# Contractions over 64 sample tokens widened to 128 rows in a hybrid encoder layer

## The chip, the core and the metric

The kernel runs on one core of a Trainium2 chip. The engines that matter here are TensorE (PE; PEld is the loading of its stationary operand, which is a separate instruction), VectorE (DVE), ScalarE (ACT), GpSimd (POOL) and SyncE (SP), which issues most of the DMAs. The metric is the device time of one execution in microseconds (us), as the median over several runs. "Rows" of a matmul are the partitions over which it contracts, "columns" the width of its stationary operand: a form such as `64*128 64x258` means 64 rows, 128 stationary columns and 258 streamed columns.

## What is computed

One layer over 256 prompt tokens and 64 sample tokens, in float32. Only the parts with a contraction over tokens matter here:

```python
def step(carry, xs):                      # mLSTM, block by block, 4 heads
    ...
    s = jnp.einsum('bhtd,bhsd->bhts', qb, kb) * jnp.exp(d - m_t[..., None])
    num = (w_inter[..., None] * jnp.einsum('bhtd,bhde->bhte', qb, C)
           + jnp.einsum('bhts,bhse->bhte', s, vb))
    ...
    C_new = decay[..., None, None] * C + jnp.einsum('bhs,bhsd,bhse->bhde', ws, kb, vb)
    n_new = decay[..., None] * n + jnp.einsum('bhs,bhsd->bhd', ws, kb)

def token_mix(...):
    ...
    zr = zs.reshape(B, nch, lc, N_GROUPS_S, GS_W)          # lc = 128 prompt, 64 sample
    mix = (jnp.einsum('gts,bnsge->bntge', w_s, zr) + ...)
    y_s = (u * mix.reshape(B, S, D_S)).astype(h.dtype)
    out = jnp.concatenate([y_m, y_s], axis=-1) @ w_out

def layer(...):
    x = x + mix
    hid = jnp.square(jax.nn.relu(rmsnorm(x, g_norm2) @ w_ff1))
    x = x + hid @ w_ff2
```

## The kernel before

Activations lie feature-major, 128 features on the partitions and 320 tokens along them (256 prompt tokens, then 64 sample tokens). Weights are the stationary operand. Each float32 operand of a projection is split into a high and a low part and a product is carried by three passes, so one output tile of 128 features takes 48 matmuls of 320 columns (`Job.matmuls`, L86 to L97): two halves of 16 (L93, L94) and 8 (L97).

The program is one list of jobs, one per output tile: 8 of z, 4 of q, 8 of v, 8 of o, 8 of u, 16 of the output projection (`out`), then four times 16 of the first and 16 of the second feed-forward matrix. All engines run what was recorded for them in the order of the code; nothing reorders it. Ahead of a job's matmuls `run_side` advances what was put off with `later`: the side work of earlier jobs, which is where all small matmuls stand. So PE's stream is: a few small matmuls, 48 projection matmuls, a few small ones, and so on. Weight halves are loaded four ahead (SP) and split two jobs ahead (ACT writes the high part, DVE the low part).

The small matmuls take the tokens in three groups, `TOK = ((0, 128), (128, 128), (256, 64))`. The third group is the sample, 64 tokens. They are:

- `z_side` (L382): transposes gz to token-major (`zt`, L391), normalises, and keeps the result in zs; zs[2] is the sample's, 64 rows of one half of the tile z2g. The other half of z2g, zs[3], takes a gain vector by DMA. z2g has a slot that held input tiles (xraw) before.
- `mix` (L413, called ahead of each u job): for each of 8 channel tiles three matmuls into one PSUM tile (L417), the third over the sample's 64 rows. They are float32, so each is two passes on PE.
- `v_side` (L448): transposes v (`vt`, L452) and splits it into vau_h and vau_l, 128 x 3 x 258, two buffers each; the third slice is the sample's, 64 rows.
- `head` (L464), one per head, in three steps with jobs between them. Step one makes the scores S (L467 to L469) and transposes k (`kt`, L472), and ACT and DVE make from them the operands Ph, Pl (448 columns, the last 64 the sample's) and kh, kl (three slices). Step two multiplies them with v (`mv`, three passes by L496 to L498): into T[0] and T[1] for the prompt; into T[2] for the sample, after a matmul of qi with the old state C0 (L507); into cs for the prompt's new state, and cs2 for the sample's. Then DVE and ACT make a normalised output hmt (L532). Step three transposes hmt back to feature-major (`hT`, L543), two halves of three transposes, the third of each over the sample's 64 rows.

Ph, Pl, kh, kl and hmt are taken from a pool with one buffer in each head. POOL sums the squares of the input early (until 42.3 us), then fills some constants (L238 to L242), sums the squares of z (L375, L378, one per z job), and makes qi.

Of the kernel before, what the change touches and what calls it, by code (L numbers as in the profile page):

```python
"""mLSTM / spatial-gating hybrid encoder layer on one core.

Activations stay feature-major ([128 features, k tile, 320 tokens]); weights are the
stationary operand. Every float32 operand of a projection is split exactly into two
float32r parts (12 significant bits each) and a product is carried by three passes
(hi*hi + hi*lo + lo*hi), accumulated in float32 in PSUM.
"""
# [10 lines left out]
F32 = mybir.dt.float32  # L18
F32R = mybir.dt.float32r
AF = mybir.ActivationFunctionType  # L20
ALU = mybir.AluOpType
PSUM = bass.MemoryType.PSUM
DRAM = bass.MemoryType.DRAM

P = 128
# [3 lines left out]
NS = 64  # L29
NT = NP + NS  # L30
H = 4
DV = 256
VA = DV + 1
VP = DV + 2
# [12 lines left out]
def emit(tc, A):  # L47
    nc = tc.nc
    act, dve, pe, pool, sp = nc.scalar, nc.vector, nc.tensor, nc.gpsimd, nc.sync
# [17 lines left out]

# [1 line left out]
    class Job:  # L69
# [28 lines left out]

# [1 line left out]
    cst = cp.tile([P, 64], F32, name="cst")  # L100
# [16 lines left out]
    def rsqrt_to(out, ss, n, tmp, tag):  # L117
        """out = (ss / n) ** -0.5, one Newton step after the table."""
        r0, t = tmp(tag + "r"), tmp(tag + "t")
        act.activation(r0, ss, AF.Abs_reciprocal_sqrt, scale=1.0 / n)  # L120
        dve.tensor_tensor(t, r0, r0, ALU.mult)
        dve.scalar_tensor_tensor(t, ss, -0.5 / n, t, ALU.mult, ALU.mult)
        dve.scalar_tensor_tensor(out, t, 1.5, r0, ALU.add, ALU.mult)

    ap_ctx = ExitStack()
    ap = ap_ctx.enter_context(tc.tile_pool(name="phase_a", bufs=1))
# [4 lines left out]

    # slots of the later Y operands that hold early intermediates
    def yslot(part, k, name, dt=F32):
# [5 lines left out]

# [1 line left out]
    nchunk = (KT + XC - 1) // XC  # L141
# [24 lines left out]
    ident = cp.tile([P, P], F32, name="ident")  # L166
# [9 lines left out]
    for k in range(KT):  # L176
# [10 lines left out]
        hi = wp.tile([P, W0], F32R, tag="hi", name=f"w0hi{k}")  # L187
        lo = wp.tile([P, 4 * P], F32R, tag="lo", name=f"w0lo{k}")
# [17 lines left out]
        first, last = k == 0, k == KT - 1  # L206
# [8 lines left out]

    # remaining constants of the first part
    C0 = ap.tile([P, H, VP], F32, name="C0")
# [8 lines left out]

# [1 line left out]
    qT = [yslot("h", 8 + h, f"qT{h}") for h in range(H)]  # L228
# [8 lines left out]
    for i in range(2):  # L237
        pool.memset(vau_h[i].bitcast(F32)[:, :, DV:VA], 1.0)  # L238
        pool.memset(vau_h[i].bitcast(F32)[:, :, VA:], 0.0)
        pool.memset(vau_l[i].bitcast(F32)[:, :, DV:], 0.0)  # L240
    gmT = ap.tile([P, 3, 36], F32, name="gmT")
    pool.memset(gmT[:], 0.0)  # L242
# [19 lines left out]
    def split_to(dst, k, src):  # L262
        """dst[k] = (hi, lo) of the float32 tile src, in the Y slots."""
        h_ = yslot("h", k, f"Yh{k}", F32R)
        l_ = yslot("l", k, f"Yl{k}", F32R)
        act.copy(h_[:], src)  # L266
        dve.tensor_tensor(l_[:], src, h_.bitcast(F32)[:], ALU.subtract)  # L267
        dst[k] = (h_, l_)

# [1 line left out]
    def row(i, name, n=4):  # L271
# [93 lines left out]

# [1 line left out]
    def z_evac(c):  # L367
# [14 lines left out]
    def z_side(c, gz):  # L382
        if c == 0:
            z01 = ap.tile([P, 2, 8, P], F32, tag="big", name="z01", bufs=2)
            z2g = ap.tile([P, 2, 8, P], F32, tag="big", name="z2g", bufs=2)
            zs[:] = [z01[:, 0], z01[:, 1], z2g[:, 0], z2g[:, 1]]
            zs.append(z01)
            sp.dma_start(zs[3], A["gsgu"].partition_broadcast(P))
        pt = sdt(f"zt{c}")
        for j, (t0, n) in enumerate(TOK):  # L390
            pe.transpose(pt[:n, P * j:P * j + P], gz[:, t0:t0 + n], ident[:])  # L391
        dve.tensor_copy(zs[4][:, :, c, :], pt[:, 0:256].rearrange("p (j c) -> p j c", c=P))
        dve.tensor_copy(zs[2][:NS, c, :], pt[:NS, 256:384])
        if c < 7:
            return
        yield
        st = sdt("ssz")
        for j, (t0, n) in enumerate(TOK):
            pe.matmul(st[:n, 2 * j:2 * j + 2], sacc[:, t0:t0 + n], ones[:, 0:2], start=True, stop=True)
        s3 = small(P, 3)("z3s")  # L400
        pool.memset(s3, 1.0)
        for j, (t0, n) in enumerate(TOK):
            dve.tensor_copy(s3[:n, j:j + 1], st[:n, 2 * j:2 * j + 1])
        rsqrt_to(rz[:], s3, D // 2, small(P, 3), "rz")
        for j, (t0, n) in enumerate(TOK):
            yield
            dve.scalar_tensor_tensor(zs[j][:n], zs[j][:n], rz[:n, j:j + 1], zs[3][:n],
                                     ALU.mult, ALU.mult)
        sp.dma_start(A["zs_out"], zs[2][:NS])
# [3 lines left out]
    def mix(c):  # L413
        g = c // 2
        pt = sdt(f"mix{c}")
        for j, (t0, n) in enumerate(TOK):
            pe.matmul(pt[:, t0:t0 + n], zs[j][:n, c, :], wsp[:n, g, :n], start=True, stop=True)  # L417
        m = tmp320(f"mixb{c}")
        dve.tensor_tensor(m[:, 0:128], pt[:, 0:128], bsp[:, g, :], ALU.add)
        dve.tensor_tensor(m[:, 128:256], pt[:, 128:256], bsp[:, g, :], ALU.add)  # L420
        dve.tensor_tensor(m[:, 256:NT], pt[:, 256:NT], bsp[:, g, :NS], ALU.add)
        mixb[c] = m
# [9 lines left out]

# [1 line left out]
    def q_evac(h):  # L434
# [29 lines left out]
    def head(h):  # L464
# [14 lines left out]
        pool.tensor_tensor(qi[:], q[:, NP:], eb[:, 192:256], ALU.mult)  # L479
        Ph = ap.tile([P, 448], F32R, tag="Ph", name=f"Ph{h}", bufs=1)  # L480
        Pl = ap.tile([P, 448], F32R, tag="Pl", name=f"Pl{h}", bufs=1)
        for n, c in ((P, slice(0, 384)), (NS, slice(384, 448))):
            act.copy(Ph[:n, c], Pm[:n, c])
            dve.tensor_tensor(Pl[:n, c], Pm[:n, c], Ph.bitcast(F32)[:n, c], ALU.subtract)
        kh = ap.tile([P, 3, P], F32R, tag="kh", name=f"kh{h}", bufs=1)
        kl = ap.tile([P, 3, P], F32R, tag="kl", name=f"kl{h}", bufs=1)
        for j, (n, e, c) in enumerate(((128, ea, 255), (128, eb, 127), (64, eb, 191))):
# [7 lines left out]
        def mm3(out, wh, wl, xh, xl, start, stop):  # L495
            pe.matmul(out, wh, xh, start=start, stop=False)  # L496
            pe.matmul(out, wh, xl, start=False, stop=False)
            pe.matmul(out, wl, xh, start=False, stop=stop)  # L498

        def mv(out, wh, wl, sl, n, j, start, stop):  # L500
            mm3(out, wh[(slice(0, n),) + sl], wl[(slice(0, n),) + sl], vh[:n, j, :], vl[:n, j, :],
                start, stop)

        mv(T[0][:, :VP], Ph, Pl, (slice(0, 128),), P, 0, True, True)
        mv(T[1][:, :VP], Ph, Pl, (slice(128, 256),), P, 0, True, False)
        mv(T[1][:, :VP], Ph, Pl, (slice(256, 384),), P, 1, False, True)
        pe.matmul(T[2][:NS, :VP], qi[:], C0[:, h, :], start=True, stop=False)  # L507
        mv(T[2][:NS, :VP], Ph, Pl, (slice(384, 448),), NS, 2, False, True)
        cs = sdt(f"cs{h}")
        mv(cs[:, :VP], kh, kl, (0,), P, 0, True, False)  # L510
        mv(cs[:, :VP], kh, kl, (1,), P, 1, False, True)
        cs2 = sdt(f"cs2{h}")
        mv(cs2[:, :VP], kh, kl, (2,), NS, 2, True, True)
        sm = small(P, 3)
# [14 lines left out]
        dve.tensor_tensor(rs, rs, den, ALU.mult)  # L529
        hmt = ap.tile([P, 3, DV], F32, tag="hm", name=f"hm{h}", bufs=1)  # L530
        for j, (t0, n) in enumerate(TOK):
# [8 lines left out]
        for e in range(2):  # L540
            pt = sdt(f"hT{h}_{e}")
            for j, (t0, n) in enumerate(TOK):
                pe.transpose(pt[:, t0:t0 + n], hmt[:n, j, e * P:e * P + P], ident[:n, :n])  # L543
            t = yslot("h", 2 * h + e, f"hmT{h}_{e}")
            act.activation(t[:], pt[:, :NT], AF.Copy, scale=gmh(2 * h + e))
            hm[h] = hm[h] or [None, None]
            hm[h][e] = t
# [18 lines left out]

# [1 line left out]
    jobs = []  # L568
# [17 lines left out]

# [1 line left out]
    xres = [None] * KT  # L588
# [111 lines left out]

# [1 line left out]
    job, xl = jobs[-1], xres[KT - 1]  # L702
# [59 lines left out]
    k = 0  # L762
# [95 lines left out]
```

## Time and profile before

| | |
|---|---|
| time, median of three runs | 1371.12 us (1370.93 to 1371.53) |
| profiled execution: span from first to last instruction | 1368.3 us |
| outside the span, against the median | 2.8 us |
| PE busy | 99% of the span, 9197 matmul passes |
| DVE, ACT, POOL busy | 50%, 39%, 4% |
| DMA | 207 MB, 151 GB/s over the span |

Of the profiled execution the profile gives the span alone; its own full time is not known, so the span is compared with the median of the runs. In the timelines a row has a start, a length (from the first start to the last end of what is merged in it), the engine, the line, the operation and the form. Consecutive matmuls overlap in the pipeline: a pass has a duration of about 0.27 to 0.31 us, and the next starts 0.11 to 0.15 us after it. So the pace of PE is read from start to start.

### The profile page before, as it was taken

Reading aid. Unit: us, or ns where it says so; the run is one execution under the profiler, and the core shown is the slowest. Engines: PE = TensorE matmul, PEld = TensorE weight load, DVE = VectorE, ACT = ScalarE, POOL = GpSimd, SP = SyncE. Lnnn points to the kernel's source line nnn. Section 1 sums busy time; section 2 is a strip of 40 time slices with the busy share of each in tenths; the row PEclk is TensorE's granted clock in tenths of the full one; section 3 lists DMA queues with packets and bytes.
Section 4 is the critical chain, followed back from the end, with each engine's and each line's share of the span. In section 5 each row is a group of like instructions: output and inputs, shape, how many; then the busy total and the mean of one; then the engine's idle time right before and its main releaser. Section 6 shows DMA issues by size and latency. Waiting matters only on the chain.

```text
span 1368.3 us, 22113 instructions
## 1 busy us (share of the span) xinstructions
PE 1355.5 (99%) x9197; PEld 1340.9 (98%) x9197; DVE 688.9 (50%) x967; ACT 538.1 (39%) x751; POOL 52.3 (4%) x79
## 2 busy tenths in 40 slices
PE   9999999999999999999999999999999999999997
PEld 8899999999999999999999999999999999999997
DVE  8785555555555544433444443344444334444444
ACT  5544454533444443333244333334432333444331
POOL 9310000000000000000000000000000000000000
PEclk9999999999999999999999999999999999999998
DMA  6745534444644444444444444444444444444432
GB/s 216 240 142 179 151 108 131 133 143 133 226 146 147 143 154 154 154 154 146 148 140 154 154 154 153 147 139 148 154 155 153 153 150 137 147 153 155 153 124 77
DMA packets 60023, 207.04 MB, mean 151 GB/s; under 512 B 6592, under 2 KB 9024, under 8 KB 59924
## 3 DMA queue, kind: packets, MB, share of 16 engines
q1 hardware_dynamic: 56932, 199.43, 45.3%
q10 hardware_dynamic: 2960, 6.17, 1.2%
q8 instruction: 72, 1.18, 0.3%
q14 instruction: 27, 0.22, 0.0%
q0 software_dynamic: 32, 0.03, 0.0%
HBM read 201.67 MB, written 3.94 MB: 150 GB/s over the span
## 4 chain that ended last, share of the span: by engine, by line
PE 95%; DVE 2%; DMA 1%; issue 1%; ACT 0%; SPq 0%; DVEq 0%; ACTq 0%
PE acc_f L94 22%; PE acc_f L93 22%; PE acc_f L97 22%; PE acc_out L94 3%; PE acc_out L97 3%; PE acc_out L93 3%; PE acc_u L93 1%; PE acc_o L93 1%; PE acc_v L97 1%; PE acc_v L93 1%; PE acc_u L94 1%; PE acc_o L97 1%; PE acc_u L97 1%; PE acc_v L94 1%; PE acc_o L94 1%; PE acc_z L93 1%
## 5 line engine op out<-in xcount | busy, mean ns | idle before, releaser
L83 DVE TENSOR_TENSOR lo_f<-raw_f,hi_f 128x1024 fp32r<-128x1024 f32 x256 | 306.1, 1221 | 139.3 <-ACT hi_f L82 137.4
L82 ACT CAST hi_f<-raw_f 128x1024 fp32r<-128x1024 f32 x256 | 260.9, 1048 | 237.4 <-PE acc_f L94 237.4
L93 PE MATMUL acc_f<-x2h,hi_f 128*128 128x320 f32 x1024 | 302.7, 310 | 0.0
L94 PE MATMUL acc_f<-x2l,hi_f 128*128 128x320 f32 x1024 | 302.4, 309 | 0.0
L93 PE MATMUL acc_f<-Yh,hi_f 128*128 128x320 f32 x1008 | 297.7, 309 | 0.0
L94 PE MATMUL acc_f<-Yl,hi_f 128*128 128x320 f32 x1008 | 297.7, 309 | 0.0
L94 PEld LDWEIGHTS acc_f<-x2l,hi_f 128*128 128x128 f32 x1024 | 192.3, 188 | 0.1
L93 PEld LDWEIGHTS acc_f<-x2h,hi_f 128*128 128x128 f32 x1024 | 192.3, 188 | 0.1
L94 PEld LDWEIGHTS acc_f<-Yl,hi_f 128*128 128x128 f32 x1008 | 189.3, 188 | 0.0
L93 PEld LDWEIGHTS acc_f<-Yh,hi_f 128*128 128x128 f32 x1008 | 189.3, 188 | 0.0
L97 PE MATMUL acc_f<-x2h,lo_f 128*128 128x320 f32 x1024 | 171.0, 309 | 0.0
L97 PE MATMUL acc_f<-Yh,lo_f 128*128 128x320 f32 x1008 | 168.4, 309 | 0.0
L97 PEld LDWEIGHTS acc_f<-x2h,lo_f 128*128 128x128 f32 x1024 | 155.4, 188 | 0.0
L97 PEld LDWEIGHTS acc_f<-Yh,lo_f 128*128 128x128 f32 x1008 | 153.0, 188 | 0.0
L644 ACT ACTIVATE f<-f 128x320 f32<-128x320 f32 x64 | 30.2, 472 | 262.6 <-DVE f L643 262.6
L650 DVE TENSOR_TENSOR xres<-acc_f,xres 128x320 f32<-128x320 f32 x63 | 31.0, 492 | 142.2 <-PE acc_f L97 142.2
L643 DVE SCALAR_TENSOR_TENSOR f<-acc_f,R 128x320 f32<-128x320 f32 x64 | 31.5, 492 | 136.8 <-PE acc_f L97 136.6
L93 PE MATMUL acc_out<-Yh,hi_out 128*128 128x320 f32 x256 | 75.6, 309 | 0.0
L94 PE MATMUL acc_out<-Yl,hi_out 128*128 128x320 f32 x256 | 75.6, 309 | 0.0
L267 DVE TENSOR_TENSOR Yl<-f,Yh 128x320 fp32r<-128x320 f32 x64 | 31.5, 492 | 65.9 <-ACT Yh L266 65.9
L94 PEld LDWEIGHTS acc_out<-Yl,hi_out 128*128 128x128 f32 x256 | 48.1, 188 | 0.0
L93 PEld LDWEIGHTS acc_out<-Yh,hi_out 128*128 128x128 f32 x256 | 48.0, 188 | 0.0
(325 smaller groups left out, 1667.7 us busy)
## 6 DMA issues: line engine op xcount, KB each, us to landing
raw_f<-w_ff SPq DMA_DIRECT2D x256, 512.0 KB, 4.0
raw_out<-w_out SPq DMA_DIRECT2D x32, 512.0 KB, 4.4
raw_z<-w_z SPq DMA_DIRECT2D x16, 512.0 KB, 5.0
raw_v<-w_v SPq DMA_DIRECT2D x16, 512.0 KB, 5.5
raw_o<-w_o SPq DMA_DIRECT2D x16, 512.0 KB, 4.9
raw_u<-w_u SPq DMA_DIRECT2D x16, 512.0 KB, 4.2
w0raw<-w SPq DMA_DIRECT2D x15, 306.0 KB, 3.0
raw_q<-w_q SPq DMA_DIRECT2D x8, 512.0 KB, 4.4
```

Source lines behind the costliest of these rows:

```text
L82: act.copy(hi[:], raw[:])
L83: dve.tensor_tensor(lo[:], raw[:], hi.bitcast(F32)[:], ALU.subtract)
L93: pe.matmul(o, self.hi[h][:, k, :], xh, start=(h == 0 and k == 0), stop=False)
L94: pe.matmul(o, self.hi[h][:, k, :], xl, start=False, stop=False)
L97: pe.matmul(o, self.lo[h][:, k, :], xh, start=False, stop=(h == 1 and k == 7))
L267: dve.tensor_tensor(l_[:], src, h_.bitcast(F32)[:], ALU.subtract)
L643: dve.scalar_tensor_tensor(t[:], acc, 0.0, R2[:], ALU.max, ALU.mult)
L644: act.activation(t[:], t[:], AF.Square)
L650: dve.tensor_tensor(xres[m], acc, xres[m], ALU.add)
```

## The change

Every matmul and transpose whose contraction runs over the 64 sample tokens takes all 128 rows. The operands' upper 64 rows are zeros. They are written once on POOL: the third slices of vau_h and vau_l and the operands Ph, Pl, kh, kl and hmt ahead of the heads, zs[2] at the first `z_side`. So that the zeros stay, Ph, Pl, kh, kl and hmt become fixed tiles, one each, which all heads write, and each head still writes only the lower 64 rows of the sample's part. The transposes of hmt use the whole identity and write 128 columns, of which only the first 64 are read. The mix takes all rows of zs[2] and of the masked spatial weights, whose upper rows meet zeros.

```diff
+        pool.memset(vau_h[i].bitcast(F32)[NS:, 2, :], 0.0)
+        pool.memset(vau_l[i].bitcast(F32)[NS:, 2, :], 0.0)
+
+    Ph = ap.tile([P, 448], F32R, name="Ph")
+    Pl = ap.tile([P, 448], F32R, name="Pl")
+    kh = ap.tile([P, 3, P], F32R, name="kh")
+    kl = ap.tile([P, 3, P], F32R, name="kl")
+    hmt = ap.tile([P, 3, DV], F32, name="hmt")
+    for t in (Ph, Pl):
+        pool.memset(t.bitcast(F32)[NS:, 384:], 0.0)
+    for t in (kh, kl):
+        pool.memset(t.bitcast(F32)[NS:, 2, :], 0.0)
+    pool.memset(hmt[NS:, 2, :], 0.0)
...
             zs.append(z01)
+            pool.memset(zs[2][NS:], 0.0)
             sp.dma_start(zs[3], A["gsgu"].partition_broadcast(P))
...
         for j, (t0, n) in enumerate(TOK):
-            pe.matmul(pt[:, t0:t0 + n], zs[j][:n, c, :], wsp[:n, g, :n], start=True, stop=True)
+            pe.matmul(pt[:, t0:t0 + n], zs[j][:, c, :], wsp[:, g, :n], start=True, stop=True)
...
-        Ph = ap.tile([P, 448], F32R, tag="Ph", name=f"Ph{h}", bufs=1)
-        Pl = ap.tile([P, 448], F32R, tag="Pl", name=f"Pl{h}", bufs=1)
...
-        kh = ap.tile([P, 3, P], F32R, tag="kh", name=f"kh{h}", bufs=1)
-        kl = ap.tile([P, 3, P], F32R, tag="kl", name=f"kl{h}", bufs=1)
...
-        def mv(out, wh, wl, sl, n, j, start, stop):
-            mm3(out, wh[(slice(0, n),) + sl], wl[(slice(0, n),) + sl], vh[:n, j, :], vl[:n, j, :],
+        def mv(out, wh, wl, sl, j, start, stop):
+            mm3(out, wh[(slice(None),) + sl], wl[(slice(None),) + sl], vh[:, j, :], vl[:, j, :],
                 start, stop)
...
-        mv(T[2][:NS, :VP], Ph, Pl, (slice(384, 448),), NS, 2, False, True)
+        mv(T[2][:NS, :VP], Ph, Pl, (slice(384, 448),), 2, False, True)
...
-        mv(cs2[:, :VP], kh, kl, (2,), NS, 2, True, True)
+        mv(cs2[:, :VP], kh, kl, (2,), 2, True, True)
...
-        hmt = ap.tile([P, 3, DV], F32, tag="hm", name=f"hm{h}", bufs=1)
...
             for j, (t0, n) in enumerate(TOK):
-                pe.transpose(pt[:, t0:t0 + n], hmt[:n, j, e * P:e * P + P], ident[:n, :n])
+                pe.transpose(pt[:, t0:t0 + P], hmt[:, j, e * P:e * P + P], ident[:])
```

The queues of DVE, ACT and SP keep their instructions and their order. On PE the order stays too and the shapes change. At the third step of head 2, ahead of an o job, PE had this (line, operation, what it writes and reads, rows and columns of the output):

```order
L97 MATMUL acc_o_2466<-xh_102,lo_o_1_2281 128x320
L543 MATMUL hT_0_2530<-ident,hm_2450 128x128 x2
L543 MATMUL hT_0_2530<-ident,hm_2450 128x64
L543 MATMUL hT_1_2536<-ident,hm_2450 128x128 x2
L543 MATMUL hT_1_2536<-ident,hm_2450 128x64
L452 MATMUL vt_2542<-ident,vT_2395 128x128 x2
L452 MATMUL vt_2542<-ident,vT_2395 64x128
L467 MATMUL S_2550<-qT_587,kT_591 128x256
```

Now it has:

```order
L97 MATMUL acc_o_2466<-xh_102,lo_o_1_2286 128x320
L552 MATMUL hT_0_2530<-ident,hmt 128x128 x3
L552 MATMUL hT_1_2536<-ident,hmt 128x128 x3
L466 MATMUL vt_2542<-ident,vT_2396 128x128 x2
L466 MATMUL vt_2542<-ident,vT_2396 64x128
L481 MATMUL S_2550<-qT_587,kT_591 128x256
```

The third transpose of each half now writes 128 columns as the other two. On POOL, behind the input's sums of squares, the added fills stand so (fills of vauh, vaul and others; sacc is the sum of squares of z):

```order
 L239 MEMSET vauh_600 128x3
 L240 MEMSET vaul_602 128x3x2
+L241 MEMSET vauh_600 64x258
+L242 MEMSET vaul_602 64x258
 L238 MEMSET vauh_601 128x3
 L239 MEMSET vauh_601 128x3
 L240 MEMSET vaul_603 128x3x2
```

Behind the second pair, `vauh_601` and `vaul_603`, follow those of Ph, Pl, kh, kl and hmt, and further down z2g's, which stands between two sums:

```order
L253 MEMSET hmt 64x256
L255 MEMSET gmT 128x108
L388 TENSOR_SCALAR sacc<-sacc 128x320
L391 TENSOR_TENSOR sacc<-sacc,zr_804 128x320
L401 MEMSET z2g 64x1024
L391 TENSOR_TENSOR sacc<-sacc,zr_887 128x320
```

So ten instructions are added to POOL's queue, nine ahead of the first sum of squares of z and one behind the second of these rows.

## Rows read from the trace of the kernel before

**Rows 1.** The page's part 1: each engine's busy time, share, instructions.

```profile
PE 1355.5 (99%) x9197; PEld 1340.9 (98%) x9197; DVE 688.9 (50%) x967; ACT 538.1 (39%) x751; POOL 52.3 (4%) x79
```

**Rows 2.** Waits of PE: total us, times, longest.

```profile
PE acc_z L93 <- DVE g L283: 1.8, 1, 1.8
...
```

**Rows 3.** Timeline of PE, head 2, step two: start us, length us, instructions.

```profile
208.26 0.65 PE L507 MATMUL T<-C,qi 128*64 128x258 f32 x2
208.84 0.33 PE L496 MATMUL T<-vauh,Ph 64*64 64x258 f32 x1
209.01 0.28 PE L497 MATMUL T<-vaul,Ph 64*64 64x258 f32 x1
209.13 0.28 PE L498 MATMUL T<-vauh,Pl 64*64 64x258 f32 x1
209.34 0.39 PE L496 MATMUL cs<-vauh,kh 128*128 128x258 f32 x1
...
210.04 0.28 PE L498 MATMUL cs<-vauh,kl 128*128 128x258 f32 x1
210.25 0.38 PE L496 MATMUL cs<-vauh,kh 64*128 64x258 f32 x1
210.47 0.28 PE L497 MATMUL cs<-vaul,kh 64*128 64x258 f32 x1
...
210.81 0.55 PE L452 MATMUL vt<-ident,vT 128*128 128x128 f32 x3
```

**Rows 4.** Timeline of PE, head 2, step three, and the scores of head 3.

```profile
218.23 1.16 PE L543 MATMUL hT<-ident,hm 128*128 128x128 f32 x6
...
219.70 0.60 PE L467 MATMUL S<-qT,kT 128*128 128x256 f32 x2
220.13 0.38 PE L468 MATMUL S<-qT,kT 128*128 128x128 f32 x2
220.45 0.33 PE L469 MATMUL S<-qT,kT 128*64 128x64 f32 x2
220.71 0.55 PE L472 MATMUL kt<-ident,kT 128*128 128x128 f32 x3
```

**Rows 5.** Timeline of PE, the first mix and the u job behind it.

```profile
275.38 0.60 PE L417 MATMUL mix<-wsp,z 128*128 128x128 f32 x4
275.91 0.43 PE L417 MATMUL mix<-wsp,z2g 64*128 64x64 f32 x2
276.27 0.41 PE L93 MATMUL acc_u<-xh,hi_u 128*128 128x320 f32 x1
276.52 0.31 PE L94 MATMUL acc_u<-xl,hi_u 128*128 128x320 f32 x1
276.67 0.31 PE L93 MATMUL acc_u<-xh,hi_u 128*128 128x320 f32 x1
```

**Rows 6.** Timeline of PE, a transpose of z; the last tile's sample part.

```profile
67.95 0.49 PE L391 MATMUL zt<-ident,gz 128*128 128x128 f32 x3
...
1355.52 1.06 PE L715 MATMUL acc_s<-Yh,lo_f 128*128 128x64 f32 x8
```

**Rows 7.** Timeline of POOL: two fills and the first sum of squares of z.

```profile
2.60 0.47 POOL L169 MEMSET MASK<- 128x448 f32 x1
...
45.17 0.18 POOL L242 MEMSET gmT<- 128x108 f32 x1
59.35 1.01 POOL L375 TENSOR_SCALAR sacc<-sacc 128x320 f32<-128x320 f32 x1 [14.00 <-ACT sacc L374]
```

**Rows 8.** Timeline, DVE beside POOL's fills and PE's wait; in brackets idle, releaser.

```profile
47.81 3.74 DVE L83 TENSOR_TENSOR lo_z<-raw_z,hi_z 128x1024 fp32r<-128x1024 f32 x3 [3.68 <-ACT hi_z L82]
...
53.45 0.41 PE L93 MATMUL acc_z<-xh,hi_z 128*128 128x320 f32 x1 [1.79 <-DVE g L283]
```

**Rows 9.** Timeline of ACT, the writing of hmt of head 2.

```profile
213.31 1.19 ACT L532 ACTIVATE hm<-T,h2q 128x256 f32<-128x256 f32 x3 [0.82 <-DVE h2q L529]
```

**Rows 10.** Windows: the stretch's end behind PE's last matmul (clock after POOL).

```profile
1361.00:1368.00 7.00, 0.00 (x0) 0.00 (x0) 3.65 (x11) 0.00 (x0) 0.00 (x0) 0.50 0.75 261
```

More of the change, by code (lines that the diff above doesn't have):

```diff
@@ L498, in mm3 @@
             pe.matmul(out, wl, xh, start=False, stop=stop)
-        def mv(out, wh, wl, sl, n, j, start, stop):
-            mm3(out, wh[(slice(0, n),) + sl], wl[(slice(0, n),) + sl], vh[:n, j, :], vl[:n, j, :],
+        def mv(out, wh, wl, sl, j, start, stop):
+            mm3(out, wh[(slice(None),) + sl], wl[(slice(None),) + sl], vh[:, j, :], vl[:, j, :],
                 start, stop)
-        mv(T[0][:, :VP], Ph, Pl, (slice(0, 128),), P, 0, True, True)
-        mv(T[1][:, :VP], Ph, Pl, (slice(128, 256),), P, 0, True, False)
-        mv(T[1][:, :VP], Ph, Pl, (slice(256, 384),), P, 1, False, True)
+        mv(T[0][:, :VP], Ph, Pl, (slice(0, 128),), 0, True, True)
+        mv(T[1][:, :VP], Ph, Pl, (slice(128, 256),), 0, True, False)
+        mv(T[1][:, :VP], Ph, Pl, (slice(256, 384),), 1, False, True)
         pe.matmul(T[2][:NS, :VP], qi[:], C0[:, h, :], start=True, stop=False)
-        mv(T[2][:NS, :VP], Ph, Pl, (slice(384, 448),), NS, 2, False, True)
+        mv(T[2][:NS, :VP], Ph, Pl, (slice(384, 448),), 2, False, True)
         cs = sdt(f"cs{h}")
-        mv(cs[:, :VP], kh, kl, (0,), P, 0, True, False)
-        mv(cs[:, :VP], kh, kl, (1,), P, 1, False, True)
+        mv(cs[:, :VP], kh, kl, (0,), 0, True, False)
+        mv(cs[:, :VP], kh, kl, (1,), 1, False, True)
         cs2 = sdt(f"cs2{h}")
-        mv(cs2[:, :VP], kh, kl, (2,), NS, 2, True, True)
+        mv(cs2[:, :VP], kh, kl, (2,), 2, True, True)
         sm = small(P, 3)
```

## The prediction

> **What bounds the kernel now.** First the busy shares [rows 1]: the matmul engine PE is busy 99% of the 1368.3 us span, DVE half of it, ACT 39%, POOL 4%. Then PE's waits [rows 2]: that view has four lines, of 1.8 us and less, and only the shown one lies between the first group of matmuls and the last tile. So from 53.45 us [rows 8] to the end of the feed-forward part PE never waits for another engine, and the time changes by what PE's own stream loses or gains. Last the timeline of PE, read by the distance from one start to the next, since durations overlap. Where a row merges n passes, the step inside it is (length − one pass's duration) / (n − 1), the duration being about 0.27 for small passes. In [rows 3] the three passes into T[2], 258 columns each, follow at 0.12 us. Transposes contracting over 128 rows follow at (0.49 − 0.27)/2 = 0.11 [rows 6], passes of 128 rows and 64 columns at (1.06 − 0.28)/7 = 0.11 [rows 6], projection matmuls of 320 columns at 276.67 − 276.52 = 0.15 [rows 5]. These are the steps at which PE runs when nothing disturbs it.
>
> **Where it is disturbed.** From cs to cs2 in [rows 3] type, columns and stationary width stay; only the contraction goes from 128 rows to 64. The step into cs2 (210.04 to 210.25) is 0.21 and the step after its first pass 0.22, against 0.12. The same pair appears on leaving 64 rows. So each change of height costs about 0.09 before the first pass of the new height and 0.05 to 0.10 behind it. It does not matter there that 64 rows are less work. A change of width does the same for a plain matmul, 128 to 64 stationary columns, as in T[1] to qi, which this change leaves alone; not for a transpose: zt's third is 128*64 and the three still keep the 0.11 step [rows 6].
>
> **Part 1, T[2] and cs2 of each head (4 heads, 6 matmuls each).** From [rows 3]. After the change T[2] is 128*64, the same as the qi passes ahead of it, and cs2 is 128*128 as cs.
> - qi to T[2]: 0.58 for two passes. Without a change of height the step out of qi is shorter by what such an exit costs elsewhere, 209.13 to 209.34 = 0.21 against 0.12: saves 0.09.
> - first T[2] step, 0.17 to 0.12: 0.05.
> - T[2] to cs still changes, in width instead of in height and width: 0 taken. Nearest row for that exit: S to kt, 220.45 to 220.71 = 0.26 for two passes at 0.11 [rows 4], a loss of 0.04 where T[2] loses 0.09, so up to 0.05 more may come.
> - cs to cs2, 0.21 to 0.12: 0.09. First cs2 step, 0.22 to 0.12: 0.10. The next two, 210.47 to 210.81, 0.34 to 0.24: 0.10.
> - the vt transposes behind it, (0.55 − 0.27)/2 = 0.14 instead of 0.11, twice: 0.06.
> Sum 0.49 a head; bounds 0.35 (if qi to T[2] still pays, for its change of type) and 0.54. I take 0.49, because cs to cs2 shows height alone to be enough. Head 3 has a projection behind it instead of vt; I take the same. 4 × 0.49 = **1.96 us**.
>
> **Part 2, the transposes of hmt (4 heads, two of 64 rows each).** In [rows 4] six transposes and three vt take 218.23 to 219.70 = 1.47; at the step of 0.109, nine take 0.98. The widened ones stream 128 columns instead of 64, and 0.11 is the step of transposes of 128 columns, so the added columns are in it. 0.49 a head, 4 × 0.49 = **1.96 us**.
>
> **Part 3, the mixes (8, each with one 64-row matmul of two passes).** [rows 5]: from the first pass to the third projection matmul, 275.38 to 276.67 = 1.29. After: six passes at 0.11 and two steps of 0.15 = 0.96. 8 × 0.33 = **2.64 us**. A pass of 128 rows and 64 columns has its own row at 0.11 [rows 6].
>
> **Part 4, ten fills more on POOL.** Nine stand among the old ones, of which the last, gmT, ended at 45.35 [rows 7]; one of 64x1024 (z2g) stands in the queue between the second and the third sum of squares. From two fills [rows 7], 0.18 for 108 columns and 0.47 for 448, I estimate 0.09 + 0.00085 per column: 4 × 0.31 (258 columns), 2 × 0.14, 2 × 0.20 and 0.31 (hmt), 2.2 us together, and 0.96 for z2g. Behind them on POOL stands the sum of squares at 59.35, which had idled 14.00 before [rows 7]; DVE, which might feel POOL's writes, is idle until 47.81 [rows 8], and the fills end at about 47.6. So 0 on the path. Without this cover it is 2.2 us, and at POOL's slowest rate in these rows (1.01 us for 320 columns, [rows 7]) 1672 and 1024 columns would take 5.3 + 3.2 = 8.5 us.
>
> The fixed tiles add no wait: Ph, Pl, kh, kl and hmt had one buffer before, so a head's first write already waited for the readers of the head before. DVE's, ACT's and SP's queues keep their order. What is late next? hmt is written by 213.31 + 1.19 = 214.50 and its transpose starts at 218.23 [rows 4, 9], 3.7 us of room where PE gains at most half a microsecond between the two; the weight halves are split as PE frees their buffers, so they move with it.
>
> **Sum.** 1.96 + 1.96 + 2.64 = 6.56 us, all on PE's own stream. The profiled span of 1368.3 becomes 1361.7. The median of the three runs lies 2.8 above the span, and I leave that as it is: 1371.12 − 6.56 = 1364.56, rounded to **1364.5 us**, 0.48% less.
>
> **Rivals.**
> - *Only part comes.* The places do not all give: if T[2] pays as before and the 2.2 us of fills come onto the path, 4 × 0.35 + 1.96 + 2.64 − 2.2 = 3.8, 1367.3; with the fills alone, 1366.8. For it: DVE's start at 47.81 comes close behind the estimated end of the fills. Against: PE's only wait ends at 53.45 [rows 8], behind a chain of DVE work that starts with that 47.81, which itself waits for ACT [rows 8].
> - *Nothing comes: a full-height load hides no longer.* If the load of a stationary operand ran beside a matmul only where their rows differ, each of the 48 widened passes (24 + 8 + 16) would show its load, 1340.9/9197 = 0.146 us [rows 1]: 7.0 us, against 6.56 saved: 1371.6. Against it: loads are busy 98% and matmuls 99% of the same span [rows 1], and 128*128 follows 128*128 at 0.11 to 0.15, so full-height loads do run beside full-height matmuls. [...]
> - *Slower: the fills hold DVE.* Place: 45 to 54 us. If POOL's fills run at the slow rate and DVE cannot work beside them, all 8.5 us come behind PE's wait at 53 us; from 6.6 us on the kernel is slower, at the full price 1371.12 − 6.56 + 8.5 = 1373.1. If PE, idle so long, also falls to the lower clock, as it does in the tail (0.50 of full, PE without work, [rows 10]), 24 matmuls of a half tile at double their 0.147 are 3.5 more: 1376.6. For it: these fills stand where PE's one wait is prepared. Against: the fills of [rows 7] themselves ran at a third of that rate.
>
> **Chances.** The forecast (1363.6 to 1365.3) 0.87; only part, 1365.3 to 1368.3, 0.06; nothing 0.05; slower 0.02. A measurement of this kernel tells 0.2%, 2.7 us, from no change. So faster 0.93, same 0.05, slower 0.02. The range runs from 1363.6 (0.05 more at each of four T[2] exits, half the runs' spread of 0.6, and 0.4 for steps that the rows give to 0.01 us) to 1366.8 (the first fills wholly on the path).
>
> **What would show it.** In the changed profile the steps into and out of the third mix operand, cs2 and the third hT should be 0.11 to 0.12, as their neighbours; six mix passes to the third projection matmul 0.96 instead of 1.29; hT to S 0.98 instead of 1.47; qi to cs about 0.94 instead of 1.08. The waits of PE should still have four lines, and the one at 53 us still 1.8. I am wrong if one of these places keeps its 0.2 us step at 128 rows (then height was not the cause), if the wait at 53 us has grown by about as much as is missing, or if the places shrank as said and the end did not move (then something else sets PE's pace).

## The result and the profile after

The changed kernel took 1363.58 us, the median of four runs (1362.65 to 1364.83), beside 1371.03 for the kernel before: a ratio of 0.9948 (95% interval 0.9934 to 0.9962). The forecast was 1364.5; the profiled span is 1361.2, against the 1361.7 of the sum. So the median came 0.9 us, the span 0.5 us below. Where the 7.1 us of span went can be read in one stretch, from the first transpose of z, behind PE's one wait, to the first matmul of the output projection, ahead of the feed-forward part. It holds all the small matmuls that changed. Timeline of PE, kernel before:

```profile
60.59 0.49 PE L391 MATMUL zt<-ident,gz 128*128 128x128 f32 x3
...
339.72 0.31 PE L93 MATMUL acc_out<-Yh,hi_out 128*128 128x320 f32 x1
```

and after:

```profile
60.45 0.49 PE L405 MATMUL zt<-ident,gz 128*128 128x128 f32 x3
...
332.67 0.31 PE L93 MATMUL acc_out<-Yh,hi_out 128*128 128x320 f32 x1
```

279.13 became 272.22, 6.91 us less; the start of the stretch moved by 0.14. This stretch is the yardstick of the experiments, as the whole time moves by 2 us and more between executions of one kernel (last section).

Inside it, the places of [rows 3 to 5]. Timeline of PE after, head 2, step two:

```profile
205.89 0.28 PE L508 MATMUL T<-vauh,Pl 128*128 128x258 f32 x1
206.10 0.65 PE L517 MATMUL T<-C,qi 128*64 128x258 f32 x2
206.68 0.33 PE L506 MATMUL T<-vauh,Ph 128*64 128x258 f32 x1
206.85 0.28 PE L507 MATMUL T<-vaul,Ph 128*64 128x258 f32 x1
206.97 0.28 PE L508 MATMUL T<-vauh,Pl 128*64 128x258 f32 x1
207.08 0.28 PE L506 MATMUL cs<-vauh,kh 128*128 128x258 f32 x1
207.20 0.29 PE L507 MATMUL cs<-vaul,kh 128*128 128x258 f32 x1
...
207.69 0.28 PE L508 MATMUL cs<-vauh,kl 128*128 128x258 f32 x1
207.81 0.28 PE L506 MATMUL cs<-vauh,kh 128*128 128x258 f32 x1
207.93 0.28 PE L507 MATMUL cs<-vaul,kh 128*128 128x258 f32 x1
...
208.18 0.49 PE L466 MATMUL vt<-ident,vT 128*128 128x128 f32 x3
```

The steps into cs2 (207.69 to 207.81) and behind its first pass are 0.12, where [rows 3] have 0.21 and 0.22, and the three vt behind it are back at (0.49 − 0.27)/2 = 0.11. But from qi to T[2] there are still 0.58, and 0.17 behind; in their place the steps from T[2] to cs have gone, 0.11 and 0.12 for 0.21 and 0.22. Timeline of PE before, the second pass into cs, behind the 209.34 of [rows 3]:

```profile
209.56 0.29 PE L497 MATMUL cs<-vaul,kh 128*128 128x258 f32 x1
```

Step three, and the first mix with the projection behind it:

```profile
215.54 0.81 PE L552 MATMUL hT<-ident,hmt 128*128 128x128 f32 x6
...
216.52 0.60 PE L481 MATMUL S<-qT,kT 128*128 128x256 f32 x2
```

```profile
271.06 0.60 PE L431 MATMUL mix<-wsp,z 128*128 128x128 f32 x4
271.50 0.33 PE L431 MATMUL mix<-wsp,z2g 128*128 128x64 f32 x2
271.64 0.39 PE L93 MATMUL acc_u<-xh,hi_u 128*128 128x320 f32 x1
...
272.02 0.31 PE L93 MATMUL acc_u<-xh,hi_u 128*128 128x320 f32 x1
```

hT to S takes 0.98 (1.47 in [rows 4]), six mix passes to the third projection matmul 0.96 (1.29 in [rows 5]). The fills on POOL, timeline after:

```profile
46.94 0.31 POOL L253 MEMSET hmt<- 64x256 f32 x1
47.30 0.19 POOL L255 MEMSET gmT<- 128x108 f32 x1
59.22 1.01 POOL L388 TENSOR_SCALAR sacc<-sacc 128x320 f32<-128x320 f32 x1 [11.72 <-ACT sacc L387]
...
64.97 0.96 POOL L401 MEMSET z2g<- 64x1024 f32 x1
```

The fills ahead of the first sum of squares of z end at 47.49, and POOL then still idles 11.72 us, 14.00 before [rows 7]; z2g's took the estimated 0.96. DVE and PE behind them, in one timeline of both:

```profile
47.67 3.74 DVE L83 TENSOR_TENSOR lo_z<-raw_z,hi_z 128x1024 fp32r<-128x1024 f32 x3 [3.61 <-ACT hi_z L82]
...
53.31 0.41 PE L93 MATMUL acc_z<-xh,hi_z 128*128 128x320 f32 x1 [1.72 <-DVE g L296]
```

DVE's three splits take 3.74 as in [rows 8], and PE's wait is 1.7 instead of 1.8. The waits of PE still have four lines.

### The profile page after: what moved, and what is told of

It reads as the page before. It is cut to its first block, busy times and chain, and to the rows that moved or that the text cites. A ratio compares the mean times of both kernels' runs of the same rounds, so it can differ in the third digit from the quotient of the medians.

```text
span 1361.2 us, 22124 instructions
## 1 busy us (share of the span) xinstructions
PE 1348.5 (99%) x9197; PEld 1339.1 (98%) x9197; DVE 688.3 (51%) x967; ACT 539.6 (40%) x751; POOL 55.4 (4%) x89
## 4 chain that ended last, share of the span: by engine, by line
PE 95%; DVE 2%; issue 1%; DMA 1%; SPq 0%; ACT 0%; DVEq 0%; ACTq 0%
PE acc_f L93 22%; PE acc_f L94 22%; PE acc_f L97 22%; PE acc_out L93 3%; PE acc_out L97 3%; PE acc_out L94 3%; PE acc_u L93 1%; PE acc_v L97 1%; PE acc_o L97 1%; PE acc_v L93 1%; PE acc_o L93 1%; PE acc_u L97 1%; PE acc_o L94 1%; PE acc_v L94 1%; PE acc_u L94 1%; PE acc_z L93 1%
```

## The experiments

Eleven runs followed. e9 is the changed kernel itself, e10 the kernel of e8 once more; the others are made from the changed kernel. "The stretch" is the one above: 279.13 before, 272.22 after.

**e1: fixed tiles and fills, 64 rows.** The contractions of mix, T[2], cs2 and hT go back to 64 rows; the rest stays as changed.

```diff
-            pe.matmul(pt[:, t0:t0 + n], zs[j][:, c, :], wsp[:, g, :n], start=True, stop=True)
+            pe.matmul(pt[:, t0:t0 + n], zs[j][:n, c, :], wsp[:n, g, :n], start=True, stop=True)
...
-        mv(T[2][:NS, :VP], Ph, Pl, (slice(384, 448),), 2, False, True)
+        mv(T[2][:NS, :VP], Ph, Pl, (slice(384, 448),), 2, False, True, NS)
...
-        mv(cs2[:, :VP], kh, kl, (2,), 2, True, True)
+        mv(cs2[:, :VP], kh, kl, (2,), 2, True, True, NS)
...
-                pe.transpose(pt[:, t0:t0 + P], hmt[:, j, e * P:e * P + P], ident[:])
+                pe.transpose(pt[:, t0:t0 + n], hmt[:n, j, e * P:e * P + P], ident[:n, :n])
```

> The changed kernel with its fixed tiles and its ten fills, but every matmul and transpose over the sample tokens contracts over 64 rows again. Theory H (what the change gained is the steps of about 0.19 us at each change of the contraction's height on PE): nothing is gained, span 1368.3 within 1 us, ratio to the kernel before 1.000; first mix pass to third projection matmul 1.29 us, first hT to S 1.47. Rival F (the gain of 7.1 us comes from the fixed tiles or from where tiles lie): span near 1361.2, ratio 0.995, with the steps of 0.2 us still there. Rival S (the fills cost on the path): span up to 2.2 us over 1368.3.

Measured: ratio 1.0003 (0.9992 to 1.0013), the stretch 341.29 − 62.09 = 279.20. Timeline of PE, first mix:

```profile
276.95 0.60 PE L431 MATMUL mix<-wsp,z 128*128 128x128 f32 x4
277.48 0.43 PE L431 MATMUL mix<-wsp,z2g 64*128 64x64 f32 x2
...
278.24 0.31 PE L93 MATMUL acc_u<-xh,hi_u 128*128 128x320 f32 x1
```

1.29 as in [rows 5]. The fixed tiles and the fills neither gain nor cost; rivals F and S fall. The profiled span, 1369.8, is over the expected 1368.3 by 1.5, outside the stated microsecond; the whole excess lies ahead of the stretch (its start, 62.09 for 60.59), for a reason given in the last section.

**e5, e6, e7, e11: one part alone.** e1 with one widening put back: the mixes (e5), hT (e6), T[2] (e7), cs2 (e11).

> Fixed tiles and fills, and of the widenings the mixes alone (8). Theory H (each change of the contraction's height on PE costs about 0.19 us, 0.09 into it and 0.10 behind): first mix pass to third projection matmul 0.95 as in the changed kernel, hT to S 1.47 and T[2] to vt 1.68 as before; gain 8 x 0.33 = 2.7, span 1365.6 (up to 1.7 more where the granted clock falls once). Rival N (the parts are not independent, the gain comes only when no 64-row operation is left): mixes still at 1.29, span 1368.3.

> Fixed tiles and fills, and of the widenings the transposes of hmt alone (8). Theory H: hT to S 0.98 instead of 1.47, mixes and T[2] to vt as before, gain 2.0, span 1366.3 (up to 1.7 more where the granted clock falls once). Rival N: hT to S 1.47, span 1368.3. Rival C (the wider transposes pay for streaming 128 columns instead of 64): steps over 0.11, 0.03 more for each of eight, gain 1.8.

> Fixed tiles and fills, and of the widenings T[2] alone (3 passes a head). Theory W (what the changed kernel shows: qi, plain float32 of 64 columns, pays on its way out by itself, whereas the float32r passes into T[2] of 64 columns pay nothing to those of 128): qi's start to T[2] 0.58 as before, T[2]'s first step 0.17 as before, and T[2] to cs 0.12 and 0.12 instead of 0.21 and 0.22, gain 0.19 a head, 0.75 in all. The prediction's own split (P): qi to T[2] 0.49, first step 0.12, T[2] to cs 0.21 and 0.22, gain 0.14 a head, 0.56. The span tells them apart no more (1367.5 to 1367.8), the steps do.

> Fixed tiles and fills, and of the widenings cs2 alone. By the prediction's split cs to cs2, its first steps and vt behind it give 0.35 a head, 1.4 us in all; by the difference of the other single parts to the whole (6.91 - 2.70 - 2.0 - 0.75) 1.46. Stretch from z's first transpose to the output projection 279.13 - 1.46 = 277.7 us; qi to T[2] and T[2] to cs as before. If the parts were not independent, the stretch differs from that by more than 0.2.

| kernel | stretch | gain on 279.13 | predicted part |
|---|---|---|---|
| e5 mixes | 276.43 | 2.70 | 2.64 |
| e6 hT | 277.15 | 1.98 | 1.96 |
| e7 T[2] | 278.39 | 0.74 | 0.56 |
| e11 cs2 | 277.76 | 1.37 | 1.40 |
| sum of the four | | 6.79 | 6.56 |
| changed kernel | 272.22 | 6.91 | 6.56 |

The parts add up within 0.12, so rival N falls. In e6 the six transposes take 0.82 in one merged row, five steps of 0.11, so C falls: the wider output costs nothing. Timeline of PE, e6:

```profile
218.99 0.82 PE L552 MATMUL hT<-ident,hmt 128*128 128x128 f32 x6
```

The spans of e5 to e7 missed their expected values by 1.9 to 4 us; the stretch did not, and the misses lie outside it (last section). e7 shows where T[2]'s gain is, timeline of PE, head 2:

```profile
210.30 0.65 PE L517 MATMUL T<-C,qi 128*64 128x258 f32 x2
210.88 0.33 PE L506 MATMUL T<-vauh,Ph 128*64 128x258 f32 x1
211.05 0.28 PE L507 MATMUL T<-vaul,Ph 128*64 128x258 f32 x1
...
211.29 0.28 PE L506 MATMUL cs<-vauh,kh 128*128 128x258 f32 x1
211.41 0.28 PE L507 MATMUL cs<-vaul,kh 128*128 128x258 f32 x1
```

0.58 and 0.17 at qi to T[2] as before, 0.12 from T[2] to cs: theory W's steps and, with 0.74 us, its size, not the prediction's.

**e2 and e3: the changes multiplied.** The passes of cs2 stand between those of cs, at 64 rows (e2, made from e1) and at 128 (e3).

```diff
-        mv(cs[:, :VP], kh, kl, (0,), 0, True, False)
-        mv(cs[:, :VP], kh, kl, (1,), 1, False, True)
-        cs2 = sdt(f"cs2{h}")
-        mv(cs2[:, :VP], kh, kl, (2,), 2, True, True)
+        cs2 = sdt(f"cs2{h}")
+        N3 = NS
+        for i in range(6):
+            j, i3 = divmod(i, 3)
+            w, x = (kh, kh, kl)[i3], (vh, vl, vh)[i3]
+            pe.matmul(cs[:, :VP], w[:, j, :], x[:, j, :], start=i == 0, stop=i == 5)
+            if i < 3:
+                pe.matmul(cs2[:, :VP], w[:N3, 2, :], x[:N3, 2, :], start=i == 0, stop=i == 2)
```

In e3 `N3 = P`.

> As the kernel with fixed tiles and fills and 64 rows, but the three passes of cs2 (64 rows) stand each behind one of the first three of the six passes of cs (128 rows): same passes, six changes of height from T[2]'s end to vt's start instead of two inside and one at the end, so that four changes come in and one moves. Theory H: each change costs 0.19 (0.09 into it, 0.10 behind it) as before, so T[2]'s third pass to vt grows from 1.68 by 0.6 to 0.8 in each of four heads, span 1368.3 + 2.4 to 3.2 = 1370.7 to 1371.5. Rival O (the cost belongs to the 64-row operation itself, once per group of passes, not to the change): 1.68 as before, span 1368.3.

> The changed kernel with the same alternation of cs and cs2, all at 128 rows. Theory H: no change of height, so nothing: from T[2]'s third pass to the first vt 1.19 us as in the changed kernel, all steps 0.11 to 0.13, span 1361.2 within 1 us. Rival B (going from one PSUM tile to the other between passes costs something by itself): the steps grow here too, by the same 0.6 to 0.8 a head as with 64 rows.

e2, timeline of PE, head 2:

```profile
212.75 0.39 PE L525 MATMUL cs<-vauh,kh 128*128 128x258 f32 x1
213.07 0.38 PE L527 MATMUL cs<-vauh,kh 64*128 64x258 f32 x1
213.38 0.39 PE L525 MATMUL cs<-vaul,kh 128*128 128x258 f32 x1
213.70 0.38 PE L527 MATMUL cs<-vaul,kh 64*128 64x258 f32 x1
```

and e3:

```profile
207.29 0.28 PE L525 MATMUL cs<-vauh,kh 128*128 128x258 f32 x1
207.41 0.29 PE L527 MATMUL cs<-vauh,kh 128*128 128x258 f32 x1
207.53 0.29 PE L525 MATMUL cs<-vaul,kh 128*128 128x258 f32 x1
207.66 0.28 PE L527 MATMUL cs<-vaul,kh 128*128 128x258 f32 x1
```

The same passes in the same order go at 0.31 to 0.32 where every step changes the height, and at 0.12 to 0.13 where none does. Each change costs 0.19 to 0.20. The stretch of e2 is 344.73 − 62.33 = 282.40, 3.20 over e1's for 16 more changes, 0.20 each (2.4 to 3.2 was expected), and its ratio to the kernel before is 1.0027 (1.0016 to 1.0038): the 64-row kernel made slower by order alone. The stretch of e3 is 272.24. Rivals O and B fall.

**e4: 96 rows.** The sample's contractions take 96 rows instead of 128.

```diff
-            pe.matmul(pt[:, t0:t0 + n], zs[j][:, c, :], wsp[:, g, :n], start=True, stop=True)
+            pe.matmul(pt[:, t0:t0 + n], zs[j][:n + 32 * (j == 2), c, :], wsp[:n + 32 * (j == 2), g, :n],
+                      start=True, stop=True)
...
-        mv(cs2[:, :VP], kh, kl, (2,), 2, True, True)
+        mv(cs2[:, :VP], kh, kl, (2,), 2, True, True, 96)
...
+                m = n + 32 * (j == 2)
+                pe.transpose(pt[:, t0:t0 + m], hmt[:m, j, e * P:e * P + P], ident[:m, :m])
```

> The changed kernel with the sample's contractions over 96 rows instead of 128 (32 rows of zeros read instead of 64). Theory H as I put it in the prediction, any change of height costs: the steps of 0.2 us are back, first mix pass to third projection matmul 1.29, hT to S 1.47, span 1368.3. Variant R (only a height of half the array or less is another height; 96 counts as 128): as in the changed kernel, 0.95 and 0.98, span 1361.2.

Timeline of PE, first mix, and head 2's hT with S behind:

```profile
271.78 0.60 PE L431 MATMUL mix<-wsp,z 128*128 128x128 f32 x4
272.22 0.33 PE L431 MATMUL mix<-wsp,z2g 96*128 96x64 f32 x2
...
272.74 0.31 PE L93 MATMUL acc_u<-xh,hi_u 128*128 128x320 f32 x1
```

```profile
216.29 0.77 PE L554 MATMUL hT<-ident,hmt 128*128 128x128 f32 x6
...
217.23 0.60 PE L482 MATMUL S<-qT,kT 128*128 128x256 f32 x2
```

0.96 and 0.94, the stretch 333.45 − 61.28 = 272.17. Variant R holds for the heights tried: 96 rows beside 128 take no longer steps, where 64 gave 1.29 and 1.47. H as the prediction put it ("only the contraction goes from 128 rows to 64") was meant for any other number and is too wide.

**e8 and e10: the narrow plain float32 matmuls widened too.** qi gets 64 columns of zeros, Ph and Pl too for T[2], and the sample's part of S takes a zero-padded copy of kT.

```diff
+    qis = [ap.tile([P, P], F32, name=f"qis{i}") for i in range(2)]
+    ks = [ap.tile([P, P], F32, name=f"ks{h}") for h in range(2)]
+    for t in qis + ks:
+        pool.memset(t[:, NS:], 0.0)
...
-        pe.matmul(s[:NS, 384:448], k[:, 256:320], q[:, 256:320], start=True, stop=True)
+        pe.matmul(s[:, 384:448], ks[h % 2][:], q[:, 256:320], start=True, stop=True)
...
-        pe.matmul(T[2][:NS, :VP], qi[:], C0[:, h, :], start=True, stop=False)
-        mv(T[2][:NS, :VP], Ph, Pl, (slice(384, 448),), 2, False, True)
+        pe.matmul(T[2][:, :VP], qi[:], C0[:, h, :], start=True, stop=False)
+        mv(T[2][:, :VP], Ph, Pl, (slice(384, 512),), 2, False, True)
```

The squares of the head's output go into its Pm instead of a tile of their own.

> The changed kernel, with the plain float32 matmuls of 64 stationary columns in the heads widened to 128 by zero columns: qi (then T[2] too) and the sample's part of S, from a zero-padded copy of kT that POOL makes ahead. Theory W (a plain float32 operand of 64 columns pays on its way in and out): T[1] to qi 0.12 instead of 0.21, qi's two passes 0.22 each, T[2] behind them at 0.12; S's third matmul at 0.11 a pass. Gain 0.28 at qi and 0.19 at S in each of four heads, 1.9 in all: span 1359.3, ratio to the kernel before 0.9935, time 1361.7. Rival T (the step from qi to T[2] belongs to the change of type from float32 to float32r): 0.31 and 0.17 stay there, gain 0.14 + 0.19 a head, 1.3. Rival D (POOL's copies or the longer Ph and Pl come onto the path): new waits of PE for POOL at S, the time as of the changed kernel or above.

Timeline of PE of e8, head 2 around qi, and S:

```profile
204.81 0.28 PE L517 MATMUL T<-vauh,Pl 128*128 128x258 f32 x1
204.93 0.60 PE L526 MATMUL T<-C,qis 128*128 128x258 f32 x2
205.17 0.47 PE L515 MATMUL T<-vauh,Ph 128*128 128x258 f32 x1
205.47 0.28 PE L516 MATMUL T<-vaul,Ph 128*128 128x258 f32 x1
```

```profile
215.59 0.38 PE L489 MATMUL S<-qT,kT 128*128 128x128 f32 x2
215.81 0.33 PE L490 MATMUL S<-qT,ks 128*128 128x64 f32 x2
215.98 0.50 PE L493 MATMUL kt<-ident,kT 128*128 128x128 f32 x3
```

From the last pass into T[1] to T[2]'s second pass 0.66, where the changed kernel has 206.85 − 205.89 = 0.96. (The step into T[2]'s first pass is short in these records and the next one, 0.30, long, so they are read as one sum.) Four steps without a loss would be an estimated 0.12, 0.22, 0.22 and 0.12, together 0.68, as S's two plain float32 passes of 256 columns take 0.43 [rows 4]. So T falls: the type changes here too and costs nothing that this sum shows. S to kt takes 0.17 instead of 0.26 [rows 4]. The stretch is 330.80 − 60.64 = 270.16, 2.06 less than the changed kernel's, 1.9 expected. Ratio 0.9935 (0.9922 to 0.9949); PE's waits stayed four, so D falls.

e9 and e10 put the changed kernel and the wider one side by side.

> The changed kernel itself, on the same chip and in the same rounds as the wider one, for a direct comparison: ratio to the kernel before 0.995; from the first transpose of z to the output projection's first matmul 272.2 us, whatever the granted clock does at other places.

> The kernel with qi, T[2] and the sample's part of S widened as well, beside the changed kernel. From the steps seen in it (2.06 us less in the stretch from z's first transpose to the output projection) it should be 2.1 us, 0.15%, under the changed kernel, ratio to the kernel before 0.9935; if the time does not show that, its gain is lost in what the granted clock does elsewhere.

e9: 1363.99 us, ratio 0.9954 (0.9941 to 0.9967), the stretch 272.22. e10: 1362.12 us, ratio 0.9937 (0.9924 to 0.9951), the stretch 330.35 − 60.17 = 270.18. The stretch repeats to 0.02 us and e10's is 2.04 shorter. The medians differ by 1.87, the same way and about as much, and all five executions of e10 (1361.67 to 1362.71) are shorter than all five of e9 (1363.01 to 1366.31). But the two intervals against the kernel before overlap: that the wider kernel's whole time is shorter is likely, and its size is known from the stretch alone.

## Why the prediction held

*PE alone sets the time.* Right: 6.91 of the 7.1 us of span are steps on PE that went, and no new wait took their place.

*The cost is the change of height.* Right, and now shown: e1 leaves everything but the height as changed (and the output width of hT with it) and gains nothing; the passes shown of e2 and e3 differ in height alone and by 0.19 us a step. One height between was run: in e4 96 rows went at 0.96 where 64 took 1.29. A change of width alone, from T[2] to cs after the change, took 0.11 and 0.12.

*The mixes, hT and cs2.* 2.70, 1.98 and 1.37 for 2.64, 1.96 and 1.40: right, from steps that the rows give to 0.01 us.

*T[2].* This term was mis-sized, and its split was wrong. The prediction took T[2] at 128*64 for "the same as the qi passes ahead of it", and so gave 0.14 a head to qi's exit and none to T[2]'s ("still changes, in width instead of in height and width: 0 taken"). It is the other way round. qi's exit kept its 0.58 and 0.17; T[2]'s exit lost both its steps, 0.19. 0.74 us instead of 0.56 (e7): one error went up and one down, and that the sum stayed so near is luck. By the prediction's own sign, a place that keeps its step, this place spoke against it: qi to cs took 207.08 − 206.10 = 0.98 and not 0.94. What kept the step is qi's 64 columns, for with those at 128 it goes (e8). The step that failed is the sentence on width: "A change of width does the same for a plain matmul". The runs show it for plain float32 only: qi and S pay (0.21 into qi and 0.17 behind T[2]'s first pass after the change, 0.26 from S to kt; in e8 0.12 into qi, 0.66 for 0.96 around it, and 0.17), the float32r passes into T[2] at 64 columns step to 128 at 0.11. T[2] is the only float32r operand of 64 columns here, and qi was not tried as float32r, so that the type makes the difference is argued from these two places. My bound of 0.35, that the change of type may cost at qi, pointed to the right place for the wrong reason. The transposes of z pay nothing for 64 columns either, as said: zt's third has 64, and the step is (0.49 − 0.27)/2 = 0.11 [rows 6].

*The fills.* Right: estimated to end at about 47.6, ended at 47.49, and DVE started at 47.67. The slower rival did not come. Whether POOL's writes slow a busy DVE is not shown: DVE stood idle beside the nine added fills, for 3.61 us until 47.67.

*The full-height load hides no longer.* This rival fails by the rows set against it: after the change 128*128 follows 128*128 at 0.11 to 0.12 in the rows shown of cs, cs2, vt and hT.

*The range.* The span was 0.5 below the sum: 0.35 in the stretch (0.18 of it T[2]), 0.14 ahead of it. The median was 0.9 below and, at 1363.58, stands on the range's lower end. The other 0.4 is the term of 2.8 from span to median, which measured 2.4 after the change. It is no constant: each execution that has its span on record takes 1.7 to 1.8 us more than that span, and what is over this in 2.8 and 2.4 is that the median execution was longer than the profiled one. The changed kernel's profiled execution took 1362.95.

## What to carry to other kernels

Read PE from start to start: in this kernel a step of 0.2 us among steps of 0.12 on both sides of one small operation was the change of form and not work, and there were as many as the order of the passes made. Where PE sets the time and a contraction over 64 rows stands among passes of 128, it is worth padding with zeros that are written once, as the wider pass cost no more here (0.12 from start to start in cs2 at 64 rows and at 128) and the stretch lost 6.91 us; plain float32 with 64 of 128 columns likewise (2.06 us of the stretch in e8). Where padding has no room, put passes of one height together: e2 lost 3.2 us by order alone, 0.20 a change.

## What was not expected of the hardware

The granted clock falls from 1.00 to 0.50 in some runs and not in others at the same work. Windows of the kernel before and of e1 behind PE's one wait (us, then busy times and passes of PE, PEld, DVE, ACT, POOL, the granted clock, DMA share, GB/s):

```profile
54.20:57.60 3.40, 3.40 (x25) 3.40 (x24) 3.40 (x6) 0.67 (x1) 0.00 (x0) 1.00 0.80 254
```

```profile
54.20:57.60 3.40, 3.40 (x15) 3.40 (x14) 3.40 (x6) 0.69 (x1) 0.00 (x0) 0.50 0.68 242
```

PE had waited 1.8 us until 53.4 in both; in e1 it then made 15 passes where the kernel before made 25, and the stretch began 1.5 us later. In e2, e5 and e6 the stretch began 1.7 us later than in the kernel before, in e7 2.4, and the mean granted clock of the span was 0.994 to 0.996 for 0.997; I take this for the same fall. In e3 it happened in the last tile, among passes that stream 64 columns, with PE busy all the time:

```profile
1350.40:1353.00 2.60, 2.60 (x15) 2.60 (x14) 2.25 (x7) 0.00 (x0) 0.00 (x0) 0.50 0.45 153
```

The kernel before ran the same passes at 1.00 (its window 1355 to 1360). From the output projection's first matmul to the end e3 took 1363.1 − 332.89 = 1030.2 us where the kernel before took 1368.3 − 339.72 = 1028.6. For the same part e4, e5, e7, e10 and e11 took 1.3 to 2.1 us more than the kernel before, e6 0.2, at mean granted clocks of 0.994 to 0.996; I take this too for a fall of the clock. By these differences a fall costs 1.3 to 2.1 us, 0.2 in e6. The falls explain most of what the spans of e1 to e7 missed: e2 was 1.8 us over its expected span, e3 1.9, e4 2.7. In e4 and e7 the stretch began another 0.8 to 0.9 us later (61.28 for the changed kernel's 60.45, 63.00 for e1's 62.09); why is open. The times of whole executions show the same: the changed kernel's four took 1362.65 and 1362.95 at a mean granted clock of 0.997, 1364.20 and 1364.83 at 0.995. Two falls are as large as half the change's gain, so in this kernel a single whole time can't judge a microsecond, while the stretch, at a granted clock of 1.00 in the traces of the kernel before and of the changed one, repeated to 0.02. Why the clock falls in one run and not in the next was not tried.
